# The gate and up product of a SwiGLU layer as seven half-size products per block

## The chip, the cores and the metric

The kernel runs on one core of one Trainium2 chip. The metric is device microseconds of one execution. Its median before the change is 961.82 us over three runs (961.47 to 962.75).

## The reference

One layer of a streaming encoder on 512 tokens of 1024 features, in float32. A mixing sub-layer (three attentions, merged by gates) comes first and is not touched. Then the feed-forward sub-layer, with `D_FF` = 2816:

```python
h = rmsnorm(x, g_ffn_pre[l])
gu = h @ w_ffn_in[l]
f = (jax.nn.silu(gu[..., :D_FF]) * gu[..., D_FF:]) @ w_ffn_out[l]
x = x + rmsnorm(f, g_ffn_post[l])
```

The change rewrites `h @ w_ffn_in`, a product of [512, 1024] with [1024, 5632].

## The kernel before, in words

**Numbers.** Every float32 operand is split into two parts, `hi` (a cast on ScalarE, L74) and `lo` (what is left, a subtraction on VectorE, L75; `split`). A product is three matmuls: hi by hi, hi by lo, lo by hi (`passes`, L85 to L87, called through `feat_k` and `feat`).

**Tiles.** SBUF tiles of 128x1024 come from tags with a fixed number of buffers (`BUFS`): raw weights `wraw` (3) and `lraw` (2), split weights `wh`, `wl`, `lwh`, `lwl` (2 each), `h` (8), `act` (22). `load` alternates between the tags with and without the l, `parts` makes the split pair. [...]

**The feed-forward sub-layer** (`mix_out`, `ffn`). The 2816 features are 22 blocks of 128. A pair is the gate block and the up block of the same 128 features. Its weights are two loads of 512 KB, issued from SyncE; the up block's raw tile is an `lraw`.

- `mix_out` makes the product with `w_out`, normalises the result (the chain squares on ScalarE, reciprocal root on GpSimd at L238, scaling on VectorE at L248) and transposes it to `h2`: eight blocks of 128 features with 512 tokens each, hi and lo. The transposes of the first 256 tokens are done during that product; those of the second 256 (`last_h2`) are issued between matmuls in `ffn`.
- The first three pairs (`NFIRST`) have their weights split ahead of time. `ffn` runs their products for tokens 0 to 255 first, while the norms of the last tokens finish, and then the second token half. These matmuls have 256 columns.
- The other 19 pairs run 48 matmuls of 512 columns each: two blocks, eight blocks of 128 input features, three passes.
- `finish` applies Silu on ScalarE (L819), multiplies on VectorE (L820) and splits the result at once into `fT`, the operand of the second product (`tok_pair`, L731), which streams `w_ffn_out` in 22 blocks.

**Order.** TensorE's instructions run in the order in which the program writes them. On the other engines a planner at build time orders instructions by the program's order and by when it expects their inputs and tiles to be ready; on the chip each engine's queue then runs in that order. A tile is reused when all its readers are done.

Of the kernel before, what the change touches and what calls it, by code (L numbers as in the profile page):

```python
# [35 lines left out]
# First distance of each of the 16 buckets of the relative bias.  # L36
# [3 lines left out]
def rel_onehot():  # L40
    """[32, 640] one-hot of the bucket of rel = 127 - column (a constant of the shapes)."""
    rel = 127 - np.arange(REL)
    b = np.searchsorted(np.asarray(BUCKET_START), np.abs(rel), side="right") - 1
    b = b + np.where(rel > 0, 16, 0)
    return (np.arange(32)[:, None] == b[None, :]).astype(np.float32)


class Layer:
# [32 lines left out]
    def passes(self, out, pairs, first, last):  # L81
        """out (+)= sum over pairs of (stationary hi, lo, moving hi, lo)."""
        n = len(pairs)
        for i, (sh, sl, mh, ml) in enumerate(pairs):
            self.nc.tensor.matmul(out, lhsT=sh, rhs=mh, start=first and i == 0, stop=False)  # L85
            self.nc.tensor.matmul(out, lhsT=sh, rhs=ml, start=False, stop=False)  # L86
            self.nc.tensor.matmul(out, lhsT=sl, rhs=mh, start=False, stop=last and i == n - 1)  # L87

# [1 line left out]
    def load(self, src, kc, c, tag=None):  # L90
        """src: [kc*128, c] in DRAM -> float32 tile [128, kc, c]."""
        self.nw += 1
        tag = tag or ("lraw" if self.late and self.nw % 2 else "wraw")
        raw = self.big(tag, F32)[:, :kc * c]
        self.nc.sync.dma_start(raw.rearrange("p (k c) -> p k c", c=c), src.rearrange("(k p) c -> p k c", p=P))
        return raw, c

    def parts(self, raw, tags=None, eng=None):
        """(hi, lo) tiles of a loaded tile."""
        raw, c = raw  # L100
        tags = tags or (("lwh", "lwl") if self.late and self.nw % 2 else ("wh", "wl"))
        v = [self.big(t)[:, :raw.shape[1]] for t in tags]
        self.split(*v, raw, eng)
        return [x.rearrange("p (k c) -> p k c", c=c) for x in v]
# [5 lines left out]
    def fill(self, us):  # L110
        """issue queued work of about us microseconds."""
        self.owed += us
        while self.owed > 0 and self.queue:
            try:
                self.owed -= next(self.queue[0])
            except StopIteration:
                self.queue.pop(0)
        if not self.queue:
            self.owed = 0.0

    def drain(self, *gens):
        """issue all queued work up to the last of gens (all of it without gens)."""
        while self.queue and (not gens or any(g in self.queue for g in gens)):
            self.fill(1.0)

    def mix(self, a, b, n=1):
        """b, with n steps of a after each of its steps."""
        for us in b:
            yield us + sum(next(a, 0.0) for _ in range(n))
        yield from a  # L130
# [10 lines left out]
    def feat(self, out, w, acts, kc=NK, n=T, **kw):  # L141
        """out[c, n] = w^T acts, contraction over kc*128 features."""
        for k in range(kc):
            self.feat_k(out, w, acts, k, kc, n, **kw)
            if k % 2:
                yield 1.28 * n / T
# [5 lines left out]
    # Logits of 64-dim heads: hi and lo of the queries of a head fill the 128 rows of the stationary  # L152
    # operand, against the hi part of the keys in both halves; a second pass on 64 rows has the lo part
    # of the keys. The even head keeps its hi part in the lower rows, the odd one in the upper rows.
# [23 lines left out]
    def feat_tiles(self, w_src, acts, out, js, n=T, t0=0, evac=None):  # L178
        """feature-major (hi, lo) of 128-column blocks js of w_src into out[j]."""
        per = T // n  # L180
        for j in js:
            w = self.weights(w_src[:, j * P:(j + 1) * P], NK, P)
            ps = self.bank()
            yield from self.feat(ps[:, 0:n], w, acts, n=n, t0=t0)
            if evac is not None:
                out[j] = evac(ps)
                continue
            if j % per == 0:
                slot = self.big("act")
            o = (j % per) * 2 * n  # L190
            out[j] = slot[:, o:o + n], slot[:, o + n:o + 2 * n]
            self.split(*out[j], ps[:, 0:n])

    def tok_tiles(self, w_src, acts, toks, out, heads=0):
        """token-major product with [1024, 512] weights for the token tiles toks; with heads, out[t]
        is one tile of (hi, lo) per head, side by side."""
# [23 lines left out]
    def squares(self, halves, both=False):  # L220
        """[128, 2] parts of the mean square of a row, of two halves of it; on both engines if wanted."""
# [9 lines left out]
    def rstd(self, ss):  # L231
        """-2 (mean + EPS) ** -0.5 of the two parts of the mean, with one Newton step."""
        return self.rstd2(self.rstd1(ss))
# [16 lines left out]
    def normed(self, x):  # L250
        """x * rstd(x) (gain not applied)."""
# [6 lines left out]
    def run(self):  # L258
# [4 lines left out]
        with self.tc.manual_schedule(engines={mybir.EngineType.PE}):  # L263
# [6 lines left out]
            # the first 128 queries have at most 128 admissible keys: all of them are selected  # L270
# [33 lines left out]
    def setup(self):  # L304
# [11 lines left out]
        # stick-breaking: ones where key == query, sliced per query tile  # L316
# [13 lines left out]
        # relative bias by distance, times 8  # L330
# [20 lines left out]
    def transposed(self, xs, k, g, hi, lo):  # L351
        """(hi, lo) of the transposes of columns 128k.. of the token tiles xs, times the gain g."""
# [6 lines left out]
    def first(self, x, row, w_ik, w_cq):  # L359
        """h^T by halves of the tokens, with the products of the first two weight blocks after each."""  # L360
# [88 lines left out]
    def index_keys(self, cq):  # L449
        nc = self.nc  # L450
        # shared key and head weights; first block of the queries of branch C
# [37 lines left out]
    def select(self):  # L489
        """additive masks: 0 for the 128 best admissible keys of a query, -BIG elsewhere."""  # L490
# [33 lines left out]
    def values_T(self, p, b, pT):  # L524
        """transposes of the key blocks that share bank b; p[i]: [128 queries, 128(i+1) keys]."""
# [11 lines left out]
    def values(self, pT, v, h, out):  # L537
        """out^T rows of head h = V^T P^T: V hi and lo side by side as one stationary operand."""
# [19 lines left out]
    def heads(self, prob, v, out, gap, first):  # L558
        """prob(h, i): probabilities of a query tile. The products with the values of a head come one
        head later, and queued work fills the waits."""  # L560
# [116 lines left out]
    def merge(self, b, out, wu):  # L677
        """acc (+)= sigmoid(gate of branch b) * (out @ wu), per 128 output features."""
# [38 lines left out]
    def tok_pair(self, w_src, acts, nk, toks, tail=0, keep=0):  # L717
        """[len(toks)] x 2 banks: token-major product with [nk*128, 1024] weights, streamed by k; the
        last tail blocks of k go token tile by token tile, the last keep blocks stay for the next call,
        which begins with them."""  # L720
# [32 lines left out]
    def post_norm(self, ps, grow, x, store=None):  # L753
        """x += rmsnorm(ps) * grow, for two banks."""
# [16 lines left out]
    def mix_out(self):  # L771
        nc, a = self.nc, self.a
        gp = self.grow("g_mix_post", "act")
        self.h2 = [self.pair("h") for _ in range(NK)]
# [8 lines left out]
        def to_h2(pr):  # L783
            s = slice(256 * pr, 256 * pr + 256)
            for k in range(NK):
                hi, lo = self.h2[k]
                self.transposed((xn[2 * pr], xn[2 * pr + 1]), k, 16, hi[:, s], lo[:, s])
# [18 lines left out]

    def ffn(self):
        nc, a = self.nc, self.a
        w_out = a["w_ffn_out"]
        fT = []  # L810

        def products(pss, ws, halves):
            for t0, n in halves:
                for ps, w in zip(pss, ws):
                    yield from self.feat(ps[:, t0:t0 + n], w, self.h2, t0=t0, n=n)

        def finish(pss):
            sg = self.sb.tile([P, T], F32, name="silu", tag="gate", bufs=2)
            nc.scalar.activation(sg, pss[0], AF.Silu)  # L819
            nc.vector.tensor_tensor(sg, sg, pss[1], op=OP.mult)  # L820
            hi, lo = self.pair("act")
            self.split(hi, lo, sg)
            fT.append((hi, lo))
# [3 lines left out]
        for j, w in enumerate(self.first_ffn):  # L827
            u = (self.bank(), self.bank()), w
            run(products(*u, ((0, 256),)))
            first.append(u)  # L830
        pss, ws = first[0]
        for k in range(NK + 2):
            if k < NK:
                next(self.last_h2)
            if k > 1:
                for ps, w in zip(pss, ws):
                    self.feat_k(ps[:, 256:512], w, self.h2, k - 2, n=256, t0=256)
        finish(pss)
        for u in first[1:]:
            run(products(*u, ((256, 256),)))  # L840
            finish(u[0])
        for j in range(self.NFIRST, NF):
            u = (self.bank(), self.bank()), self.ffn_weights(j)
            run(products(*u, ((0, T),)))
            finish(u[0])
# [6 lines left out]
        run(self.tok_pair(w_out, fT, NF, range(NT), tail=4))  # L852
# [18 lines left out]
```

## Time and profile before

| | |
|---|---|
| median of 3 runs | 961.82 us |
| lowest and highest run | 961.47 and 962.75 us |
| span of the profiled execution, first to last instruction | 960.9 us |
| TensorE busy | 938.7 us, 98% |
| VectorE, ScalarE, GpSimd busy | 534.3, 404.6, 107.0 us |
| the 19 pairs that are rewritten | 622.11 to 832.40 us of the span |

The profile gives no time of the profiled execution but its span, which lies 0.6 to 1.9 us under the three runs. It names engines PE (TensorE matmuls), PEld (its weight loads), DVE (VectorE), ACT (ScalarE), POOL (GpSimd) and SP (SyncE). An operation is shown as line, engine, operation, written tile, read tiles and shape; "idle before" is the time that the engine stood still before it, with what ended the wait. `bank` is a PSUM tile, all others are in SBUF.

### The profile page before, as it was taken

Reading aid. Unit: us, or ns where it says so; the run is one execution under the profiler, and the core shown is the slowest. Engines: PE = TensorE matmul, PEld = TensorE weight load, DVE = VectorE, ACT = ScalarE, POOL = GpSimd, SP = SyncE. Lnnn points to the kernel's source line nnn. Section 1 sums busy time; section 2 is a strip of 40 time slices with the busy share of each in tenths; the row PEclk is TensorE's granted clock in tenths of the full one; section 3 lists DMA queues with packets and bytes.
Section 4 is the critical chain, followed back from the end, with each engine's and each line's share of the span. In section 5 each row is a group of like instructions: output and inputs, shape, how many; then the busy total and the mean of one; then the engine's idle time right before and its main releaser. Section 6 shows DMA issues by size and latency. Waiting matters only on the chain.

```text
span 960.9 us, 11731 instructions
## 1 busy us (share of the span) xinstructions
PE 938.7 (98%) x4426; PEld 760.5 (79%) x4426; DVE 534.3 (56%) x920; ACT 404.6 (42%) x705; POOL 107.0 (11%) x147
## 2 busy tenths in 40 slices
PE   5999999999999999999999999999999999999997
PEld 4967888888777777777788888988888888888885
DVE  7568999963587876667544477333333333322225
ACT  5354575432666555655443355322223223212122
POOL 4000000010022303334222102000000000000000
PEclk9999999999999999999999999999999999999999
DMA  7423542343343322122283536023333233332202
GB/s 226 124 63 103 154 138 78 99 110 110 109 134 109 99 67 77 44 56 66 73 267 99 176 106 201 1 76 101 88 101 97 88 102 97 110 106 92 66 23 87
DMA packets 129532, 98.95 MB, mean 103 GB/s; under 512 B 4652, under 2 KB 115292, under 8 KB 129476
## 3 DMA queue, kind: packets, MB, share of 16 engines
q1 hardware_dynamic: 128884, 97.16, 33.9%
q10 hardware_dynamic: 592, 1.05, 0.3%
q8 instruction: 34, 0.56, 0.2%
q14 instruction: 22, 0.18, 0.1%
HBM read 93.73 MB, written 2.12 MB: 100 GB/s over the span
## 4 chain that ended last, share of the span: by engine, by line
PE 88%; DVE 6%; issue 2%; DMA 1%; ACT 1%; POOL 1%; SPq 0%; DVEq 0%; POOLq 0%; ACTq 0%
PE bank L85 20%; PE bank L87 20%; PE bank L86 20%; PE bank L731 14%; PE bank L176 3%; DVE wl L75 3%; PE bank L531 2%; PE bank L546 2%; PE bank L175 2%; PE bank L206 1%; PE bank L208 1%; PE bank L207 1%; DMA act<-in_x_dram 1%; DVE score L503 1%; DMA lraw<-in_w_ffn_in_dram 1%
## 5 line engine op out<-in xcount | busy, mean ns | idle before, releaser
L75 DVE TENSOR_TENSOR wl<-wraw,wh 128x1024 fp32r<-128x1024 f32 (+1 forms) x131 | 155.1, 1185 | 177.6 <-ACT wh L74 173.2
L74 ACT CAST wh<-wraw 128x1024 fp32r<-128x1024 f32 (+1 forms) x131 | 127.2, 972 | 229.4 <-PE bank L86 163.1
L85 PE MATMUL bank<-h,wh 128*128 128x512 f32 (+1 forms) x528 | 209.6, 397 | 0.0
L87 PE MATMUL bank<-h,wl 128*128 128x512 f32 (+1 forms) x528 | 204.7, 388 | 1.0 <-DVE wl L75 0.9
L86 PE MATMUL bank<-h,wh 128*128 128x512 f32 (+1 forms) x528 | 204.4, 387 | 0.0
L87 PEld LDWEIGHTS bank<-h,wl 128*128 128x128 f32 x528 | 99.1, 188 | 22.0 <-DVE wl L75 1.7
L85 PEld LDWEIGHTS bank<-h,wh 128*128 128x128 f32 x528 | 99.3, 188 | 20.0 <-issue 1.2
L86 PEld LDWEIGHTS bank<-h,wh 128*128 128x128 f32 x528 | 99.4, 188 | 17.8
L74 ACT CAST lwh<-lraw 128x1024 fp32r<-128x1024 f32 x36 | 37.9, 1052 | 119.4 <-PE bank L86 76.2
L731 PE MATMUL bank<-lwh,act 128*128 128x512 f32 x240 | 72.6, 393 | 0.0
L731 PE MATMUL bank<-wh,act 128*128 128x512 f32 x240 | 72.5, 393 | 0.0
L75 DVE TENSOR_TENSOR lwl<-lraw,lwh 128x1024 fp32r<-128x1024 f32 x36 | 44.1, 1224 | 43.1 <-ACT lwh L74 41.3
L85 PE MATMUL bank<-h,lwh 128*128 128x512 f32 x152 | 60.1, 396 | 0.0
L86 PE MATMUL bank<-h,lwh 128*128 128x512 f32 x152 | 60.1, 396 | 0.0
L87 PE MATMUL bank<-h,lwl 128*128 128x512 f32 x152 | 60.1, 395 | 0.0
L238 POOL TENSOR_TENSOR rs<-ms,mhalf 128x1 f32<-128x1 f32 x18 | 10.4, 579 | 423.9 <-DVE ms L237 419.9
L820 DVE TENSOR_TENSOR silu<-silu,bank 128x512 f32<-128x512 f32 x22 | 15.1, 686 | 76.4 <-PE bank L87 73.6
L595 POOL TENSOR_TENSOR p<-toep,score 128x128 f32<-128x128 f32 (+3 forms) x32 | 29.8, 944 | 218.4 <-DVE score L504 112.3
L731 PEld LDWEIGHTS bank<-wh,act 128*128 128x128 f32 x240 | 45.1, 188 | 10.0
L731 PEld LDWEIGHTS bank<-lwh,act 128*128 128x128 f32 x240 | 45.1, 188 | 9.9
L74 ACT CAST act<-bank 64x512 fp32r<-64x512 f32 (+3 forms) x63 | 34.8, 552 | 38.1 <-DVE act L75 16.7
L85 PE MATMUL bank<-act,wh 128*128 128x512 f32 (+1 forms) x128 | 48.6, 380 | 0.0
(161 smaller groups left out, 1616.6 us busy)
## 6 DMA issues: line engine op xcount, KB each, us to landing
wraw<-in_w_in_dram SPq DMA_DIRECT2D x64, 512.0 KB, 3.5
wraw<-in_w_ffn_in_dram SPq DMA_DIRECT2D x22, 512.0 KB, 3.7
lraw<-in_w_ffn_in_dram SPq DMA_DIRECT2D x22, 512.0 KB, 3.7
wraw<-in_w_ffn_out_dram SPq DMA_DIRECT2D x11, 512.0 KB, 3.7
lraw<-in_w_ffn_out_dram SPq DMA_DIRECT2D x11, 512.0 KB, 3.4
wraw<-in_w_mem_kv_dram SPq DMA_DIRECT2D x8, 512.0 KB, 3.4
lraw<-in_w_out_dram SPq DMA_DIRECT2D x6, 512.0 KB, 6.3
wraw<-in_w_out_dram SPq DMA_DIRECT2D x6, 512.0 KB, 4.0
```

What stands on the lines that cost most here:

```text
L74: self.nc.scalar.copy(hi, src)
L75: (eng or self.nc.vector).tensor_tensor(lo, src, hi.bitcast(F32), op=OP.subtract)
L85: self.nc.tensor.matmul(out, lhsT=sh, rhs=mh, start=first and i == 0, stop=False)
L86: self.nc.tensor.matmul(out, lhsT=sh, rhs=ml, start=False, stop=False)
L87: self.nc.tensor.matmul(out, lhsT=sl, rhs=mh, start=False, stop=last and i == n - 1)
L175: self.nc.tensor.matmul(out, lhsT=x[:, s], rhs=k[h % 2][:, 0:n], start=True, stop=False)
L176: self.nc.tensor.matmul(out, lhsT=x[r, s], rhs=lo[r, 0:n], start=False, stop=True)
L531: self.nc.tensor.transpose(ps[:, c:c + P], p[i][:, j * P:(j + 1) * P], self.ident)
L546: nc.tensor.matmul(ps[:, j * P:T], lhsT=w, rhs=part[:, o:o + n], start=j == 0 and i == 0, stop=j == NT - 1 and i == 1)
L595: nc.gpsimd.tensor_tensor(s, toep[0][:, 0:n][:, ::-1], self.mask[i], op=OP.add)
L731: self.nc.tensor.matmul(ps[c], lhsT=st_[:, s], rhs=mv_[:, 0, c * 512:(c + 1) * 512], start=f and k == order[0], stop=l and k == order[-1])
L820: nc.vector.tensor_tensor(sg, sg, pss[1], op=OP.mult)
```

## The change

For pairs 3 to 21 the two products of a pair become one block product. The inputs' features are cut into halves of 512 and the tokens into halves of 256. With g0, g1 the gate block's and u0, u1 the up block's halves by features, and q(f, t) the quarters of h, the four outputs (gate and up, for each token half) come from seven products of a combined left side (128x512 weights) with a combined right side, each of 4 blocks of 128 features, three passes and 256 columns: 84 matmuls of 256 columns instead of 48 of 512. Products 1, 2 and 4 take the weights as they are; the left sides of 5, 6, 7 and 3 are sums made on GpSimd for each pair. Products 1, 2 and 3 take quarters of h as they are; the right sides of 5, 7, 6 and 4 are made once (`right_sides`: four sums hi + lo of 128x1024 on GpSimd, then a difference and a split on VectorE and ScalarE for each). Splits come per product, into one of eight 128x1024 tiles. The partial results accumulate in three banks and are read out in between (`blocks`), and the last two products of a pair run among the first of the next: in order 1, 5, 7 (of the pair before), 2, 6, 4 (before), 3.

The layout of `h2` follows: eight `h` tiles, one per quarter and part. The result of a pair stays in float32 (two pairs in one `act` tile) and is split in the second product, when a block is first used. `passes` hands on a flag that lets a matmul add to a bank whose sum was closed before. The scratch for DMAs that GpSimd would issue is made smaller. Comments are removed, and these lines are left out of the diff.

```diff
@@ mix_out
-        self.h2 = [self.pair("h") for _ in range(NK)]
+        self.hq = {(f, t): (self.big("h"), self.big("h")) for t in range(2) for f in range(2)}
+        cut = lambda x, k: x[:, 256 * (k % 4):256 * (k % 4) + 256]
+        self.h2 = [[tuple(cut(x, k) for x in self.hq[k // 4, t]) for k in range(NK)] for t in range(2)]
...
+    def right_sides(self):
+        nc, q = self.nc, self.hq
+        r = {}
+        for k, (hi, lo) in q.items():
+            r[k] = self.big("act", F32)
+            nc.gpsimd.tensor_tensor(r[k], hi.bitcast(F32), lo.bitcast(F32), op=OP.add)
+        y = {1: q[0, 0], 2: q[1, 0], 3: q[1, 1]}
+        for p, out, x, z in ((5, (0, 0), (0, 1), (0, 0)), (7, (0, 1), (1, 1), (0, 1)),
+                             (6, (1, 1), (1, 1), (0, 0)), (4, (1, 0), (1, 0), (1, 1))):
+            nc.vector.tensor_tensor(r[out], r[x], r[z], op=OP.subtract)
+            y[p] = self.big("act"), self.big("act")
+            self.split(*y[p], r[out])
+        return y
+
+    def left_sides(self, j):
+        nc = self.nc
+        (g, _), (u, _) = (self.load(self.a["w_ffn_in"][:, c:c + P], NK, P) for c in (j * P, DFF + j * P))
+        x = {1: g[:, 0:512], 2: g[:, 512:1024], 4: u[:, 512:1024]}
+        for p, a, b, op in ((5, u[:, 0:512], x[4], OP.add), (6, 5, 1, OP.subtract),
+                            (7, x[1], u[:, 0:512], OP.subtract), (3, 2, 6, OP.subtract)):
+            a, b = (x[i] if isinstance(i, int) else i for i in (a, b))
+            x[p] = self.late.tile([P, 512], F32, name="sum", tag="sum", bufs=6)
+            nc.gpsimd.tensor_tensor(x[p], a, b, op=op)
+        return x
+
+    def product(self, out, x, y, first):
+        self.nq += 1
+        t = self.big(("wh", "lwh", "wl", "lwl")[self.nq % 4])
+        hi, lo = t[:, 0:512], t[:, 512:1024]
+        self.split(hi, lo, x)
+        for k in range(4):
+            a, b = slice(k * P, k * P + P), slice(k * 256, k * 256 + 256)
+            self.passes(out, [(hi[:, a], lo[:, a], y[0][:, b], y[1][:, b])], first and k == 0, k == 3,
+                        skip_group_check=not first)
+
+    def blocks(self, js, y, out):
+        nc = self.nc
+        half = lambda name: self.late.tile([P, 256], F32, name=name, tag=name, bufs=2)
+        def begin(j):
+            x, f = self.left_sides(j), out(j)
+            px, py, pz = (self.bank()[:, 0:256] for _ in range(3))
+            s1, s2, s3 = half("s1"), half("s2"), half("s3")
+            g = self.sb.tile([P, T], F32, name="silu", tag="gate", bufs=2)
+            self.product(px, x[1], y[1], True)
+            nc.scalar.copy(s1, px)
+            self.product(pz, x[5], y[5], True)
+            nc.scalar.copy(s3, pz)
+            yield
+            self.product(py, x[2], y[2], True)
+            nc.vector.tensor_tensor(g[:, 0:256], py, s1, op=OP.add)
+            self.product(px, x[6], y[6], False)
+            nc.scalar.copy(s2, px)
+            yield
+            self.product(pz, x[3], y[3], False)
+            nc.vector.tensor_tensor(g[:, 256:512], pz, s2, op=OP.add)
+            nc.scalar.activation(g, g, AF.Silu)
+            yield
+            self.product(px, x[7], y[7], False)
+            nc.vector.tensor_tensor(s3, px, s3, op=OP.add)
+            nc.vector.tensor_tensor(f[:, 256:512], g[:, 256:512], s3, op=OP.mult)
+            yield
+            self.product(px, x[4], y[4], False)
+            nc.vector.tensor_tensor(f[:, 0:256], g[:, 0:256], px, op=OP.mult)
+            yield
+        prev = iter(())
+        for j in js:
+            g = begin(j)
+            for _ in range(2):
+                next(g)
+                next(prev, None)
+            next(g)
+            prev = g
+        for _ in prev:
+            pass
@@ ffn
-        finish(pss)
-        for u in first[1:]:
-            run(products(*u, ((256, 256),)))
-            finish(u[0])
-        for j in range(self.NFIRST, NF):
-            u = (self.bank(), self.bank()), self.ffn_weights(j)
-            run(products(*u, ((0, T),)))
-            finish(u[0])
+        finish(pss, 0)
+        y = self.right_sides()
+        for j, u in enumerate(first[1:], 1):
+            run(products(*u, 1))
+            finish(u[0], j)
+        self.blocks(range(self.NFIRST, NF), y, out)
...
+        class Parts:
+            def __getitem__(_, k):
+                if k not in pairs:
+                    pairs[k] = self.pair("act")
+                    self.split(*pairs[k], fT[k])
+                return pairs[k]
-        run(self.tok_pair(w_out, fT, NF, range(NT), tail=4))
+        run(self.tok_pair(w_out, Parts(), NF, range(NT), tail=4))
...
-    nc = bacc.Bacc("TRN2", target_bir_lowering=False, num_devices=1)
+    nc = bacc.Bacc("TRN2", target_bir_lowering=False, num_devices=1, dynamic_dma_scratch_size=1024)
```

## Rows read from the trace of the kernel before

**Rows 1.** The page: busy time, the granted clock by slices, the chain by line.
```profile
PE 938.7 (98%) x4426; PEld 760.5 (79%) x4426; DVE 534.3 (56%) x920; ACT 404.6 (42%) x705; POOL 107.0 (11%) x147
...
PEclk9999999999999999999999999999999999999999
...
PE bank L85 20%; PE bank L87 20%; PE bank L86 20%; PE bank L731 14%; PE bank L176 3%; DVE wl L75 3%; PE bank L531 2%; PE bank L546 2%; PE bank L175 2%; PE bank L206 1%; PE bank L208 1%; PE bank L207 1%; DMA act<-in_x_dram 1%; DVE score L503 1%; DMA lraw<-in_w_ffn_in_dram 1%
```

**Rows 2.** Stretches: length, busy time (records) of PE, PEld, DVE, ACT, POOL; clock; DMA.
```profile
622.11:832.40 210.29, 210.29 (x915) 171.38 (x914) 69.80 (x75) 59.73 (x76) 0.00 (x0) 1.00 0.32 95
...
832.40:948.70 116.30, 116.22 (x507) 94.73 (x506) 31.84 (x36) 23.93 (x30) 1.09 (x2) 1.00 0.23 73
```

**Rows 3.** Timeline of VectorE, 19 pairs: start us, us, operation, idle before.
```profile
633.44 0.69 DVE L820 TENSOR_TENSOR silu<-silu,bank 128x512 f32<-128x512 f32 x1 [3.58 <-PE bank L87]
...
644.51 0.69 DVE L820 TENSOR_TENSOR silu<-silu,bank 128x512 f32<-128x512 f32 x1 [3.58 <-PE bank L87]
```

**Rows 4.** Timeline of VectorE, second token half of pairs 1 and 2.
```profile
616.62 0.69 DVE L820 TENSOR_TENSOR silu<-silu,bank 128x512 f32<-128x512 f32 x1 [2.15 <-PE bank L87]
...
622.38 0.69 DVE L820 TENSOR_TENSOR silu<-silu,bank 128x512 f32<-128x512 f32 x1 [3.69 <-PE bank L87]
```

**Rows 5.** Timeline of VectorE: two operations of 512 columns in a row.
```profile
219.76 0.69 DVE L704 TENSOR_TENSOR act<-bank,gate 128x512 f32<-128x512 f32 x1 [0.64 <-PE bank L87]
220.37 0.68 DVE L75 TENSOR_TENSOR wl<-wraw,wh 128x512 fp32r<-128x512 f32 x1
```

**Rows 6.** Groups by line and form, whole span: busy us, mean ns, idle before.
```profile
L74 ACT CAST wh<-wraw 128x1024 fp32r<-128x1024 f32 x107 | 112.3, 1051 | 206.2 <-PE bank L86 145.1 <-PE bank L731 43.1 <-issue 9.7
...
L707 POOL TENSOR_TENSOR act<-act,gate 128x512 f32<-128x512 f32 x16 | 26.9, 1684 | 61.8 <-DVE gate L706 61.8
...
L74 ACT CAST act<-silu 128x512 fp32r<-128x512 f32 x22 | 13.7, 624 | 7.2 <-DVE silu L820 7.1
...
L620 POOL TENSOR_TENSOR p<-p,e 128x512 f32<-128x512 f32 x8 | 8.7, 1092 | 13.9 <-ACT vlow L549 7.5 <-DVE e L618 6.4
...
L75 DVE TENSOR_TENSOR pt<-bank,pt 128x256 fp32r<-128x256 f32 x16 | 6.5, 406 | 1.0 <-ACT pt L74 0.9
...
L74 ACT CAST pt<-bank 128x256 fp32r<-128x256 f32 x16 | 6.0, 374 | 4.7 <-PE bank L531 4.5
```

**Rows 7.** Timelines of GpSimd and of VectorE where both work at once.
```profile
460.28 1.29 POOL L707 TENSOR_TENSOR act<-act,gate 128x512 f32<-128x512 f32 x1 [2.00 <-DVE gate L706]
...
460.37 2.29 DVE L75 TENSOR_TENSOR wl<-wraw,wh 128x1024 fp32r<-128x1024 f32 x1 [0.16 <-ACT wh L74]
...
466.76 1.23 DVE L75 TENSOR_TENSOR wl<-wraw,wh 128x1024 fp32r<-128x1024 f32 x1
...
466.89 2.25 POOL L707 TENSOR_TENSOR act<-act,gate 128x512 f32<-128x512 f32 x1
...
581.71 2.42 POOL L75 TENSOR_TENSOR act<-lraw,act 128x1024 fp32r<-128x1024 f32 x1 [2.34 <-ACT act L74]
...
582.62 0.69 DVE L760 SCALAR_TENSOR_TENSOR prod<-bank,act 128x512 f32<-128x512 f32 x1
```

**Rows 8.** Timelines of VectorE and TensorE before the 19 pairs.
```profile
585.27 0.48 DVE L79 SCALAR_TENSOR_TENSOR h<-bank,cols,h 128x256 fp32r<-128x256 f32 x1
...
597.78 0.75 DVE L248 TENSOR_SCALAR act<-fin,rs 128x1024 f32<-128x1024 f32 x1
...
602.02 0.60 PE L356 MATMUL bank<-ident,act 128*128 128x128 f32 x4
...
609.15 0.48 DVE L79 SCALAR_TENSOR_TENSOR h<-bank,cols,h 128x256 fp32r<-128x256 f32 x1 [0.45 <-ACT h L78]
```

**Rows 9.** Timeline of TensorE at a wait, and the stretch after it.
```profile
585.34 0.39 PE L86 MATMUL bank<-h,act 128*128 128x256 f32 x1 [1.38 <-DVE h L79]
...
586.00:589.40 3.40, 3.40 (x18) 3.40 (x18) 3.40 (x6) 3.40 (x10) 0.00 (x0) 0.52 0.37 109
```

**Rows 10.** DMA issues of the page: count, KB each, median us to landing.
```profile
wraw<-in_w_ffn_in_dram SPq DMA_DIRECT2D x22, 512.0 KB, 3.7
```

More of the change, by code (lines that the diff above doesn't have):

```diff
@@ L79, in split_gain, with passes @@
         self.nc.vector.scalar_tensor_tensor(lo, src, g, hi.bitcast(F32), op0=OP.mult, op1=OP.subtract)
-    def passes(self, out, pairs, first, last):
+    def passes(self, out, pairs, first, last, **kw):
         n = len(pairs)
         for i, (sh, sl, mh, ml) in enumerate(pairs):
-            self.nc.tensor.matmul(out, lhsT=sh, rhs=mh, start=first and i == 0, stop=False)
-            self.nc.tensor.matmul(out, lhsT=sh, rhs=ml, start=False, stop=False)
-            self.nc.tensor.matmul(out, lhsT=sl, rhs=mh, start=False, stop=last and i == n - 1)
+            self.nc.tensor.matmul(out, lhsT=sh, rhs=mh, start=first and i == 0, stop=False, **kw)
+            self.nc.tensor.matmul(out, lhsT=sh, rhs=ml, start=False, stop=False, **kw)
+            self.nc.tensor.matmul(out, lhsT=sl, rhs=mh, start=False, stop=last and i == n - 1, **kw)
     def load(self, src, kc, c, tag=None):
@@ L783, in to_h2 @@
         def to_h2(pr):
-            s = slice(256 * pr, 256 * pr + 256)
             for k in range(NK):
-                hi, lo = self.h2[k]
-                self.transposed((xn[2 * pr], xn[2 * pr + 1]), k, 16, hi[:, s], lo[:, s])
+                self.transposed((xn[2 * pr], xn[2 * pr + 1]), k, 16, *self.h2[pr][k])
                 yield 0.25
@@ L809, in ffn, with out, products, finish @@
         w_out = a["w_ffn_out"]
[L810 to L817, printed above, removed]
+        fT, self.nq = [], 0
+        def out(j):
+            if j % 2 == 0:
+                self.slot = self.big("act", F32)
+            fT.append(self.slot[:, (j % 2) * T:(j % 2 + 1) * T])
+            return fT[j]
+        def products(pss, ws, t):
+            for ps, w in zip(pss, ws):
+                yield from self.feat(ps[:, 256 * t:256 * t + 256], w, self.h2[t], n=256)
+        def finish(pss, j):
             sg = self.sb.tile([P, T], F32, name="silu", tag="gate", bufs=2)
             nc.scalar.activation(sg, pss[0], AF.Silu)
[L820 to L823, printed above, removed]
+            nc.vector.tensor_tensor(out(j), sg, pss[1], op=OP.mult)
         run = lambda g: [None for _ in g]
@@ L828, in ffn @@
             u = (self.bank(), self.bank()), w
-            run(products(*u, ((0, 256),)))
+            run(products(*u, 0))
             first.append(u)
@@ L836, in ffn @@
                 for ps, w in zip(pss, ws):
-                    self.feat_k(ps[:, 256:512], w, self.h2, k - 2, n=256, t0=256)
-        finish(pss)
-        for u in first[1:]:
-            run(products(*u, ((256, 256),)))
-            finish(u[0])
-        for j in range(self.NFIRST, NF):
-            u = (self.bank(), self.bank()), self.ffn_weights(j)
-            run(products(*u, ((0, T),)))
-            finish(u[0])
+                    self.feat_k(ps[:, 256:512], w, self.h2[1], k - 2, n=256)
+        finish(pss, 0)
[4 more added lines that the diff above has]
+        self.blocks(range(self.NFIRST, NF), y, out)
         gp = self.grow("g_ffn_post", "h")
@@ L851, in ffn @@
         self.done = done
-        run(self.tok_pair(w_out, fT, NF, range(NT), tail=4))
+        pairs = {}
+        class Parts:
[5 more added lines that the diff above has]
+        run(self.tok_pair(w_out, Parts(), NF, range(NT), tail=4))
 def kernel(**inputs):
-    nc = bacc.Bacc("TRN2", target_bir_lowering=False, num_devices=1)
+    nc = bacc.Bacc("TRN2", target_bir_lowering=False, num_devices=1, dynamic_dma_scratch_size=1024)
     arrays = {}
```

## Prediction

> **What bounds the kernel now.** I read the page's busy shares and its clock line first: TensorE is busy for 98% of the span, VectorE for 56%, GpSimd for 11%, and the granted clock is 0.9 or more in every slice [rows 1]. Then the chain of waits: the three lines of `passes` (L85 to L87), the body of every feature-major product, carry 60% of it [rows 1]. Then the stretches: the 19 pairs that the change rewrites take 210.29 us, from 622.11 to 832.40, with TensorE busy for all of it, VectorE for 69.80, ScalarE for 59.73 and GpSimd for nothing [rows 2]. So in this stretch one column of TensorE work removed is time removed, as long as the three other engines keep pace. Those queues, not TensorE, decide what the change is worth.
>
> One pair takes 11.07 us: the multiply that ends it (L820) starts at 633.44 and at 644.51 [rows 3], and 210.29/19 gives the same. A pair is 2 x 8 x 3 = 48 matmuls of 512 columns, so one costs 11.07/48 = 0.231 us.
>
> **What the change removes on TensorE.** Seven products, each of 4 blocks of k by 3 passes, are 84 matmuls of 256 columns. The trace has their price: pairs 1 and 2 do their second token half in 48 such matmuls each, and their closing multiplies start at 616.62 and 622.38 [rows 4], so one costs 5.76/48 = 0.120 us. A pair costs 84 x 0.120 = 10.08 us, 0.99 less than now. Seven eighths of the columns would give 1.38; the smaller matmul has more overhead per column (0.120 for half of 0.231), which takes back 0.39. If nothing else binds, 19 pairs gain 18.8 us. The weight loads go with the matmuls: in that stretch they have the same pitch, so they are in the 0.120.
>
> **What it adds on the other engines, per pair.** VectorE: seven `lo` subtractions of 512 columns (now two of 1024 in the pair), and five operations of 256 columns: three additions and one multiply that read PSUM, one multiply that reads SBUF alone. A 512 operation shows 0.69 us, but the next starts 0.61 after it [rows 5]; the 256 one shows 0.406 [rows 6], less the same 0.08 is 0.33. Sum: 7 x 0.61 + 5 x 0.33 = 5.92 us, against 69.80/19 = 3.67 now. ScalarE: seven casts at 0.62, three PSUM copies at 0.37 and one Silu at about 0.62 [rows 6] are 6.1 us, against 3.14 now; that lies under 10.08. Loads stay two of 512 KB a pair.
>
> GpSimd gets four sums of 128x512. The cheapest such group is 1.09 (a multiply), the dearest mean is 1.68 [rows 6], which contains waiting; a sum that started without a wait shows 1.29, and half of the 1024 subtraction (2.42) is 1.21 [rows 7]. I take 1.28, by the first: 5.12 us a pair.
>
> 5.92 and 5.12 look small beside 10.08, but they exclude each other in part. Rows 7 show it. A `lo` subtraction of 1024 takes 1.23 when it comes first (466.76); started 0.09 after a GpSimd sum it took 2.29, and it ended 1.09 after the sum's end (462.66 against 461.57). The other way round, the sum that met the subtraction of 466.76 took 2.25 for its 1.29, and ended 1.15 after it. While GpSimd ran for 2.42 us from 581.71, the VectorE operation at 582.62 that reads a PSUM bank kept its usual 0.69. So VectorE work with both inputs in SBUF and GpSimd work take turns; VectorE work with a PSUM input does not. [...]
>
> VectorE's queue is my main term. [...] If no GpSimd work lies beside VectorE work, a pair needs 5.92 + 5.12 = 11.04 us; if all four PSUM-reading operations (1.32) lie beside a sum, 9.72. The middle is 10.38, which is over TensorE's 10.08. Nothing in rows says how well the planner packs them, and the seven subtractions outnumber the four operations that can overlap, so I take 10.38: a gain of 0.69 a pair, 13.1 us for 19. The ends are 11.04 (gain 0.6 in all) and the bound by TensorE (18.8). Eight tiles for split sides let the splits run up to eight products (11.5 us) ahead, which can hide part of a deficit of 0.30 x 19 = 5.7 us; how full that store is at the start depends on the next part.
>
> **Edits at the edges.** (a) `right_sides` puts four GpSimd sums of 1024 (2.42 each) in the queue that also makes the reciprocal root of the mix's last norms. Two of them are ready when the first token half is split (585.7), in the middle of the chain through three such roots to the scaled rows at 598.53; TensorE has other products until 602.02 [rows 8]. Two sums in front cost that chain 4.84 at most, the slack is 602.02 - 598.53 = 3.5: 0 to 1.3 us, I take 0.5. (b) The second half is complete at 609.63 [rows 8]. From there the first made side needs a sum, a difference, a cast and a subtraction (2.42 + 1.23 + 1.05 + 1.23 = 5.9 [rows 6, 7], with the other sum ahead of it 8.3), so it is ready by 618, and product 5 starts at 622.11 + 1.44 = 623.5: hidden. The third made side (product 6) needs both sums and six VectorE operations, 12.2 us, plus the first blocks' splits and sums between them (up to 5 x 0.61 + 4 x 1.28 = 8.2): 622 to 630 against 626.4. 0 to 3.6, I take 1. This also leaves the store half full. (c) After the last pair, products 7 and 4 follow each other with a VectorE addition from their bank between: 0.41 and two hand-overs, 0.5. (d) The 22 splits of the product's result move into the second FFN product, where VectorE is busy for 31.84 of 116.30 and ScalarE for 23.93 [rows 2]: 22 x 0.69 and 22 x 0.62 fit, cost 0; uncovered, the first would cost 1.3 once. (e) The new layout of h2, the matmul flag, the smaller scratch (no DMA is issued from GpSimd) and the removed comments: 0. Edges: 2.0.
>
> Sum: 961.8 - 13.1 + 2.0 = 950.7, say **951**. The profiled execution's span is 960.9, the runs 961.47 to 962.75; the sum is a difference and I lay it on the median.
>
> **The rivals.** *TensorE stays fed* (the store and the overlap suffice): 961.8 - 18.8 + 0 to 2 = 943 to 945. For it: with the best packing the two engines need 9.72 of 10.08. Against: that is 96% of the time, with jitter.
>
> *No overlap*: 11.04 a pair, 961.8 - 0.6 + 2 = 963, no change. For it: the stretched subtraction waited for almost the whole sum. Against: it needs every PSUM-reading operation to fall outside the sums.
>
> [...]
>
> *The lookahead is not there.* The `u` block's raw tile has two buffers and is held until the split for product 4, six places into the next pair's order. [...]
>
> **Chances.** The forecast, 10.2 to 10.9 a pair with the edges (947 to 960): 0.50. TensorE fed: 0.25. No overlap: 0.10. Clock: 0.10. No lookahead: 0.05. The range takes in the fed case and most of the no-overlap case, 942.5 to 964. A measurement of this kernel can tell about 0.2% (1.9 us) from no change. Faster: 0.50 + 0.25 + about 0.05 of the others = 0.80; same: 0.07 (the middle of no overlap); slower: 0.13 (the clock, most of the lookahead case).
>
> **What would show it.** In the profile after: TensorE's 256-column matmuls at a pitch of 0.120, and seven products per pair; the pair's period from its last multiply between 10.08 and 10.9; `lo` subtractions of 512 stretched to 1.2 to 1.9 in every pair, beside GpSimd sums; TensorE waiting for VectorE's `lo` by some tenths of a us per pair; clock 0.9 throughout. The prediction is wrong if the sums are much cheaper or dearer than 1.28, if TensorE waits for ScalarE or for a load, if the wait sits at the start (622 to 630), or if the clock falls inside the 19 pairs.

## The result and the profile after

The median after is 1011.08 us (1010.01 to 1011.57) against 962.23 us before on the same chip: a ratio of 1.0514, interval 1.0499 to 1.0529. The forecast of 951 and its range were wrong, and so was the sign. The profiled execution took 1010.88 us with a span of 1009.1, 48.2 more than the span before.

The page after, busy time, granted clock, and the chain of waits by engine and by line; it answers to [rows 1]:

```profile
PE 939.6 (93%) x5110; PEld 797.2 (79%) x5110; DVE 650.2 (64%) x1099; ACT 461.6 (46%) x861; POOL 229.1 (23%) x227
...
PEclk9999999999999999999999998988999998999999
...
PE 62%; DVE 14%; DMA 9%; issue 8%; POOL 4%; ACT 3%; POOLq 0%; DVEq 0%; SPq 0%; ACTq 0%
PE bank L731 14%; PE bank L85 12%; PE bank L87 11%; PE bank L86 11%; DMA lraw<-in_w_ffn_in_dram 9%; DVE wl L75 3%; PE bank L176 3%; POOL sum L839 3%; PE bank L531 2%; PE bank L546 2%; DVE lwl L75 2%; PE bank L175 1%; DVE wh L75 1%; DVE lwh L75 1%; PE bank L206 1%
```

TensorE has less of the chain now, 62%. The lines of `passes` had 60% of it and now have 34%; the loads of the `u` blocks into `lraw` have 9%, the GpSimd sums 3%, and VectorE 14% (here `g` and `u` are the gate and the up block of a pair). Stretches of the kernel after come next (length, then busy time and records of TensorE, its weight loads, VectorE, ScalarE, GpSimd; granted clock; DMA): up to the transposes of the second token half, from there to the first block product, and the 19 pairs.

```profile
580.00:611.29 31.29, 21.86 (x155) 20.24 (x153) 26.23 (x37) 12.61 (x30) 21.26 (x16) 0.92 0.26 77
...
611.29:632.18 20.89, 20.89 (x157) 20.89 (x157) 11.92 (x15) 9.86 (x14) 4.77 (x2) 0.88 0.02 4
...
632.18:880.54 248.36, 208.16 (x1598) 204.50 (x1597) 160.07 (x232) 106.93 (x214) 101.04 (x68) 0.93 0.29 85
```

The first two of them in the kernel before, with the same TensorE work:

```profile
580.00:603.49 23.49, 20.99 (x155) 19.97 (x153) 15.50 (x33) 11.68 (x26) 4.58 (x5) 0.93 0.56 163
...
603.49:622.11 18.62, 18.62 (x157) 18.62 (x158) 6.00 (x11) 7.16 (x12) 0.00 (x0) 1.00 0.00 1
```

So the 48.2 us have three places. Before the second half's transposes 31.29 - 23.49 = 7.80; from there to the pairs 20.89 - 18.62 = 2.27, in which TensorE is busy throughout, with the same 157 matmuls, at a lower granted clock (0.88 against 1.00); and 37.9 in the pairs: 248.36 against 210.4 by the same bounds ([rows 2] end at the last multiply, 0.13 earlier). The rest, from the second FFN product's first matmul to the end, is 128.6 against 128.4.

**Where the pairs lose.** TensorE is idle for 40.2 of the 248.36 us. These are the waits of the kernel after around the pairs (us in all, times, longest):

```profile
POOL sum L839 <- DMA lraw<-in_w_ffn_in_dram: 138.7, 17, 19.8
...
PE bank L85 <- DVE s L879: 40.2, 18, 4.0
```

TensorE stops once a pair, for an addition on VectorE (L879); GpSimd stops once a pair, for the load of the `u` block. The chain of waits shows one turn (start, us, what):

```profile
718.26 5.10 DMA lraw<-in_w_ffn_in_dram
...
723.53 1.27 POOL sum L839
...
724.82 0.63 ACT wh L74
...
726.61 1.75 DVE lwh L75
...
731.31 0.60 DVE wh L75
...
731.94 4.66 DMA lraw<-in_w_ffn_in_dram
```

It goes from load to load, and TensorE is not in it. VectorE's timeline shows what stands between the first split that needs the load and the split that lets the next load start; its first line is the same last split one turn earlier:

```profile
717.56 0.68 DVE L75 TENSOR_TENSOR lwh<-lraw,lwh 128x512 fp32r<-128x512 f32 x1
...
725.47 1.21 DVE L75 TENSOR_TENSOR wh<-sum,wh 128x512 fp32r<-128x512 f32 x1 [5.37 <-ACT wh L74]
726.61 1.75 DVE L75 TENSOR_TENSOR lwh<-sum,lwh 128x512 fp32r<-128x512 f32 x1
728.28 0.41 DVE L879 TENSOR_TENSOR s<-bank,s 128x256 f32<-128x256 f32 x1
728.62 1.42 DVE L75 TENSOR_TENSOR wl<-wraw,wl 128x512 fp32r<-128x512 f32 x1
729.97 0.41 DVE L880 TENSOR_TENSOR act<-silu,s 128x256 f32<-128x256 f32 x1
730.30 0.41 DVE L870 TENSOR_TENSOR silu<-bank,s 128x256 f32<-128x256 f32 x1
730.63 0.68 DVE L75 TENSOR_TENSOR lwl<-sum,lwl 128x512 fp32r<-128x512 f32 x1
731.23 0.68 DVE L75 TENSOR_TENSOR wh<-lraw,wh 128x512 fp32r<-128x512 f32 x1
```

From 725.47 on, the L75 rows are the splits for product 5 of pair y, 7 of the pair before it (x), 2 and 6 of y, and last (731.23, the only one of this turn that reads `lraw`) product 4 of x. Product 4's split is the last reader of x's `u` tile, one of two, and the load into that tile is issued at 731.94. The split for product 5 of y (725.47) could not run before y's `u` block had landed. So each load waits for a split that stands in VectorE's queue behind splits that wait for the load before it: one load per turn, in a circle. The turn is load and hand-over 5.27 (718.26 to 723.53), sum and cast 1.94 (to 725.47), VectorE's rows 6.44 (to 731.91), issue 0.03: 13.68. The closing multiplies (L883) at 650.35 and 865.58 are 16 turns apart, 13.45 each on average.

The matmul that TensorE resumes with after the turn's stop is product 4's, and its own split was ready 10.5 us earlier (VectorE's row of 717.56). It waited for L879, which reads the bank that product 4 writes, and which stood in VectorE's queue behind the two late splits. The last matmul that L879 needs, product 7's, had ended at 722.46, and VectorE was idle up to 725.47; L879 still ran in its place, at 728.28:

```profile
728.75 0.39 PE L85 MATMUL bank<-act,lwh 128*128 128x256 f32 x1 [3.44 <-DVE s L879]
...
728.75:732.50 3.75, 3.75 (x18) 3.75 (x19) 3.74 (x7) 0.62 (x1) 0.74 (x1) 0.54 0.30 84
```

After the stop the granted clock is 0.54, for 18 matmuls. Inside the circle that costs nothing: the chain of the turn does not go through TensorE, which needs 10.04 of the 13.45 us when it is fed (second experiment).

### The profile page after: what moved, and what is told of

Read it like the earlier page. It is cut to its first block, busy times and chain, and to the rows that moved or that the text cites. A ratio compares the mean times of both kernels' runs of the same rounds, so it can differ in the third digit from the quotient of the medians.

```text
span 1009.1 us, 13643 instructions
## 1 busy us (share of the span) xinstructions
PE 939.6 (93%) x5110; PEld 797.2 (79%) x5110; DVE 650.2 (64%) x1099; ACT 461.6 (46%) x861; POOL 229.1 (23%) x227
## 4 chain that ended last, share of the span: by engine, by line
PE 62%; DVE 14%; DMA 9%; issue 8%; POOL 4%; ACT 3%; POOLq 0%; DVEq 0%; SPq 0%; ACTq 0%
PE bank L731 14%; PE bank L85 12%; PE bank L87 11%; PE bank L86 11%; DMA lraw<-in_w_ffn_in_dram 9%; DVE wl L75 3%; PE bank L176 3%; POOL sum L839 3%; PE bank L531 2%; PE bank L546 2%; DVE lwl L75 2%; PE bank L175 1%; DVE wh L75 1%; DVE lwh L75 1%; PE bank L206 1%
## 5 line engine op out<-in xcount | busy, mean ns | idle before, releaser
L75 DVE TENSOR_TENSOR wl<-wraw,wh 128x1024 fp32r<-128x1024 f32 (+1 forms) x112 | 131.8, 1178 | 102.8 <-ACT wh L74 98.3
L85 PE MATMUL bank<-h,wh 128*128 128x512 f32 (+2 forms) x432 | 167.2, 387 | 0.0
L87 PE MATMUL bank<-h,wl 128*128 128x512 f32 (+2 forms) x428 | 161.3, 377 | 1.0 <-DVE wl L75 0.9
L86 PE MATMUL bank<-h,wh 128*128 128x512 f32 (+2 forms) x432 | 161.5, 374 | 0.0
L85 PEld LDWEIGHTS bank<-h,wh 128*128 128x128 f32 x432 | 82.7, 191 | 13.7 <-issue 1.2
L86 PEld LDWEIGHTS bank<-h,wh 128*128 128x128 f32 x432 | 82.6, 191 | 11.6
L85 PE MATMUL bank<-act,wh 128*128 128x256 f32 (+1 forms) x204 | 71.1, 348 | 6.7 <-DVE s L879 6.7
L87 PE MATMUL bank<-act,wl 128*128 128x256 f32 (+1 forms) x208 | 69.6, 335 | 0.0
L86 PE MATMUL bank<-act,wh 128*128 128x256 f32 (+1 forms) x204 | 68.5, 336 | 0.0
L839 POOL TENSOR_TENSOR sum<-lraw 128x512 f32<-128x512 f32 x19 | 24.9, 1312 | 138.9 <-DMA lraw<-in_w_ffn_in_dram 138.9
L85 PEld LDWEIGHTS bank<-act,wh 128*128 128x128 f32 x204 | 39.2, 192 | 13.0 <-DVE s L879 7.5
L75 DVE TENSOR_TENSOR lwl<-lraw,lwh 128x1024 fp32r<-128x1024 f32 x17 | 21.3, 1254 | 36.5 <-ACT lwh L74 36.4
L620 POOL TENSOR_TENSOR p<-p,e 128x128 f32<-128x128 f32 (+3 forms) x32 | 24.3, 760 | 86.3 <-DVE e L618 43.9
```

Of the source, the lines that this page charges most:

```text
L75: (eng or self.nc.vector).tensor_tensor(lo, src, hi.bitcast(F32), op=OP.subtract)
L620: nc.gpsimd.tensor_tensor(be, be, e[:, 1:n + 1], op=OP.mult)
L839: nc.gpsimd.tensor_tensor(x[p], a, b, op=op)
```

## Experiments

The first theory is the circle. It has two rivals. The port theory, as the expectations call it, is that VectorE's subtractions and GpSimd's sums take turns: in the turn above the splits beside sums took 1.21, 1.75 and 1.42 us, the others 0.68. Only the longer times are measured; no run shows what makes the two engines take turns. The clock theory is that TensorE at a low clock (0.54 after the stop) holds the pair up. For the start the theory is that GpSimd's sums delay the last norms.

**A third buffer for `u`.** The tags swap, so that `u` has three raw tiles and `g` two. Every engine keeps the same instructions.

```diff
-        (g, _), (u, _) = (self.load(..., NK, P) for c in (j * P, DFF + j * P))
+        (g, _), (u, _) = (self.load(..., NK, P, t) for c, t in ((j * P, "lraw"), (DFF + j * P, "wraw")))
```

> The up block's raw tile takes the tag with three buffers and the gate block's the one with two; nothing else changes, every engine has the same instructions. Loop theory: the 13.45 us of a pair are a circle: the load of an up block waits for a free raw tile, which product 4's lo subtraction frees; that subtraction stands in VectorE's queue behind the next pair's subtraction for product 5, which waits for the next up load. With a third buffer two pairs share a turn of the circle, so the pair falls to 10.1 to 10.9 us and the kernel to 1011 - 18 x 2.8 = about 960 (954 to 966). Port theory: the GpSimd sums and VectorE's subtractions take turns and need 13.45 us a pair by themselves: same instructions, so 1011 within 3. [...]

965.08 us (963.57 to 966.99). The kernel before, run beside it, took 961.17; the ratio is 1.0039 (1.0026 to 1.0052). The pairs of this kernel:

```profile
637.34:834.77 197.43, 191.81 (x1598) 190.08 (x1597) 175.92 (x232) 106.26 (x214) 99.51 (x65) 1.00 0.36 107
```

One buffer more takes 50.9 us out of the pairs (10.39 each) and 46 off the run. The same sums stand beside the same subtractions, so neither the turns that the two engines take nor the amount of VectorE work is enough to make the 13.07. By the clock theory the pairs would have kept their time too; here the granted clock is 1.00. TensorE still waits 5.6 us in seven places, and the start is worse: the pairs begin at 637.34.

**Product 4's split earlier.** The split is written after product 3 of its own pair, ahead of the next pair's splits; no buffer is added. `halves` is the first part of `product`, set apart.

```diff
             self.product(pz, x[3], y[3], False)
+            x4 = self.halves(x[4])
...
-            self.product(px, x[4], y[4], False)
+            self.product(px, x4, y[4], False)
```

> Only the place of product 4's split changes: it is written right after product 3 of its own pair, ahead of the next pair's products 1 and 5, so that VectorE frees the up block's raw tile before it waits for the next up load. Buffers, engines and TensorE's order stay. Loop theory: as with the third buffer, 10.1 to 10.9 us a pair, kernel about 960 (954 to 966). Port theory and clock theory: 1011 within 4.

948.84 us in one run. The same kernel once more, with several runs:

> The early split of product 4 alone, timed in rounds: 948.8 within 2, as in its one look; 19 pairs at 190.8 us with VectorE and GpSimd taking turns all the same.

947.26 us (946.39 to 948.47), ratio 0.9860 (0.9843 to 0.9876) to 961.0: the fastest version of this study, faster than both kernels. Its pairs, and three rows of its VectorE timeline (product 4's split, the next pair's product 5, product 4's again):

```profile
625.83:816.65 190.82, 189.99 (x1599) 189.79 (x1597) 176.10 (x231) 110.52 (x216) 104.81 (x66) 1.00 0.36 107
...
704.39 1.45 DVE L75 TENSOR_TENSOR wl<-lraw,wl 128x512 fp32r<-128x512 f32 x1
...
705.95 1.60 DVE L75 TENSOR_TENSOR wh<-sum,wh 128x512 fp32r<-128x512 f32 x1
...
715.23 1.45 DVE L75 TENSOR_TENSOR lwh<-lraw,lwh 128x512 fp32r<-128x512 f32 x1
```

The split that frees the tile now precedes the one that waits for the next load, and the circle is open. TensorE is busy for 189.99 of 190.82: 10.04 a pair, its own bound. Its one stop comes after the last pair's product 7 (0.83 us at 815.11). It keeps this pace although the subtractions are still stretched (1.45 and 1.60 for 0.69) and GpSimd is busy for 104.81. Moving one split in the program, with the order that the planner makes of it, was worth 57.5 us of pairs.

The run gained 63.8, so 6.3 more came from the start, where the edit changes nothing that the program asks for. In this kernel GpSimd makes the sums of `right_sides` behind the last norms and not among them. The two VectorE operations behind the last root, those sums (L821), and the stretch from the transposes to the pairs:

```profile
604.40 0.22 DVE L243 SCALAR_TENSOR_TENSOR rt<-rs,ms 128x1 f32<-128x1 f32 x1 [0.45 <-POOL rs L238]
604.66 0.16 DVE L244 SCALAR_TENSOR_TENSOR rs<-rt,rs 128x1 f32<-128x1 f32 x1
...
609.13 9.48 POOL L821 TENSOR_TENSOR act<-h 128x1024 f32<-128x1024 f32 x4
...
607.21:625.83 18.62, 18.62 (x157) 18.62 (x157) 12.85 (x15) 9.20 (x14) 11.33 (x6) 1.00 0.02 5
```

What this says of the start is taken up below.

**The sums on VectorE.** GpSimd has nothing left in the pairs; the order and the buffers are those of the change.

```diff
-            nc.gpsimd.tensor_tensor(x[p], a, b, op=op)
+            nc.vector.tensor_tensor(x[p], a, b, op=op)
```

> The four sums of a pair run on VectorE in place of GpSimd; two buffers for the up block as in the change. Loop theory: the circle stays (load about 5, then sums at 0.6, cast, subtractions without stretches), so the pair still takes 11.3 to 12.5 us, kernel 975 to 992. Port theory: nothing excludes VectorE any more, its work is 5.9 + 2.4 = 8.4 us a pair, so TensorE is the bound at 10.1 us and the kernel falls to 945 to 955.

969.55 us in one run: between the two expectations, nearer the circle's and below its range.

```profile
627.72:838.79 211.07, 194.80 (x1599) 191.54 (x1597) 160.44 (x300) 107.50 (x215) 0.00 (x0) 0.99 0.34 100
...
753.73 0.69 DVE L839 TENSOR_TENSOR sum<-lraw 128x512 f32<-128x512 f32 x1 [2.01 <-DMA lraw<-in_w_ffn_in_dram]
```

The circle is still there: now VectorE itself waits for the load, once a pair, and a pair takes 11.11. But it is 1.96 shorter a pair than with GpSimd. So the turns between VectorE and GpSimd are no cause by themselves, but they lengthen the circle: the GpSimd sum, its hand-over and the stretched subtractions are links of it. This run does not tell them apart.

**Three `u` buffers and every sum on VectorE**, those of `right_sides` too:

```diff
-            nc.gpsimd.tensor_tensor(r[k], hi.bitcast(F32), lo.bitcast(F32), op=OP.add)
+            nc.vector.tensor_tensor(r[k], hi.bitcast(F32), lo.bitcast(F32), op=OP.add)
```

and the edits of the first and third experiments.

> Three buffers for the up block, and all sums (those of the pairs and the four of the right sides) on VectorE. Loop theory and port theory agree: the pair at TensorE's 10.1 us, and with no GpSimd work among the norms before the pairs the stretch starts at about 622 to 626 as before, so the kernel takes 943 to 952. If it stays above 962, neither theory has the cause.

957.19 us (956.45 to 959.26), ratio 0.9959 (0.9945 to 0.9973). It misses what both theories expected, in the pairs and at the start. Its stretch ahead of the pairs, and the pairs:

```profile
606.98:628.37 21.39, 21.39 (x157) 21.39 (x157) 12.95 (x17) 7.92 (x12) 0.00 (x0) 0.86 0.02 3
...
628.37:828.90 200.53, 193.57 (x1598) 190.31 (x1597) 162.34 (x299) 111.37 (x216) 0.00 (x0) 1.00 0.36 106
```

A pair takes 10.55, not 10.1: TensorE waits 6.7 us in 13 places, and VectorE's sums wait for the loads of `u` for 31.5 us in 16, with everything behind them. With three buffers the place of the sums changes little in the pairs (10.39 on GpSimd, in the first experiment); with two, VectorE was the better place (11.11 against 13.07). The pairs begin 9.0 us earlier than in the first experiment, and the run is 7.9 shorter. But the start of the kernel before did not come back: the 157 matmuls from 606.98 on took 21.39 us at clock 0.86, against 18.62 at 1.00.

**Keeping the sums out of the norms.** Two gates are tried with the early split, and the first of them on the change alone too. The first ties the loads of the pairs' first blocks to the last normed rows: a VectorE operation writes one column of the raw tile, which the load then overwrites. The second lets them load and ties their sums to those rows (first pair) or to the last split of h2 (next two): it adds zero times a value to one column of the weights. The first gate, without the lines that choose the loads:

```diff
         raw = self.big(tag, F32)[:, :kc * c]
+        if after is not None:
+            self.nc.vector.tensor_copy(raw[:, 0:1], after[:, 0:1])
```

> Two edits to the change: product 4's split early (as in the run of that edit alone), and the raw tiles of pairs 3 and 4 and of pair 5's gate block get one column from the last normalised rows before their load, so that no sum or split of the pairs can run among the norms. Start theory: the pairs began 5.6 to 15 us late because planned-ahead sums and splits stood in GpSimd's, VectorE's and ScalarE's queues among the last norms and the h2 splits; without them the first pair starts at 622 to 625 (622.11 before), the pairs take 190.8, the rest 128.4, so the kernel takes 942 to 946. Rival: the late start comes from the new layout of h2 or from the right sides, which stay: 948 to 950, as with the early split alone.

952.12 us (951.56 to 953.62), ratio 0.9911 (0.9896 to 0.9925): slower than without the gate (947.26).

> The change with the gated loads alone; product 4's split stays late. The circle through the up block's raw tile stays, so the pairs take 245 to 252 us. Start theory: first pair at 622 to 626 in place of 632.18, kernel 1001 to 1006. Rival (start held by the right sides): 1008 to 1012.

1007.94 us in one run; the pairs took 247.51, as expected with the circle, and began at 630.12.

The second gate, again the operation alone:

```diff
+                    nc.vector.scalar_tensor_tensor(raw[:, c:c + 1], z[:, 0:1], 0.0, raw[:, c:c + 1], op0=OP.mult, op1=OP.add)
```

> Product 4's split early as before; the loads of the first pairs stay early too, but a one-column operation that leaves the weights as they are makes their sums and splits wait: pair 3 for the last normalised rows, pairs 4 and 5 for the last split of h2. Start theory: the norms end near 595, as with the gated loads, and now only pair 3's six splits and four sums lie in the gap before the h2 splits, so TensorE waits under 2 us there in place of 9.34; first pair at 622 to 624, pairs 190.8, kernel 941 to 945. Rival: the right sides and the later sums collide after the h2 splits and the wait moves into the pairs: 946 to 950.

958.12 us (957.03 to 958.82), ratio 0.9965 (0.9953 to 0.9977). TensorE's waits at the start, first in the load gate's kernel, then in the sum gate's:

```profile
609.52 0.48 PE L358 MATMUL bank<-ident,act 128*128 128x128 f32 x1 [9.34 <-DVE h L79]
```

```profile
606.68 0.69 PE L356 MATMUL bank<-ident,act 128*128 128x128 f32 x2 [4.21 <-DVE h L79]
...
622.73 9.38 POOL L821 TENSOR_TENSOR act<-h 128x1024 f32<-128x1024 f32 x4
...
634.32 0.58 PE L85 MATMUL bank<-act,wl 128*128 128x256 f32 x1 [5.22 <-ACT act L74]
```

All three missed their times. With the loads gated the norms were done by 595.1, and TensorE's first stop, at 584.38, fell to 0.51 us; but the loads, sums and splits then stood in front of the splits of h2, and TensorE waited 9.34. With the sums gated, the four sums of `right_sides` ran behind sums of the pairs, 14 us later than with the early split alone (622.73 against 609.13), and a product waited 5.22 for them. The wait moved each time; no version here has the start of the kernel before (622.11; the nearest is 625.83). Which order would do it stays open.

## Why the prediction was wrong

**TensorE's part was right.** 84 matmuls at 0.120 were to be 10.08 a pair; the kernel with the early split measures 10.04 with one stop of TensorE. The 18.8 us are there: its pairs are 19.6 shorter than before.

**The main term was of the wrong kind.** The prediction took VectorE's queue and its turns with GpSimd as a rate, 10.38 a pair as the middle of 9.72 and 11.04. As a rate they do not bind: the kernel with the early split runs at 10.04, TensorE's own pace, with stretched subtractions in every pair. So the no-overlap rival (11.04) is wrong too, and "TensorE stays fed" had the pairs right once the circle was gone. What bound was a latency: 13.45 a turn, in which VectorE is idle for 5.37 us at a stretch.

**The step that failed** is how the lookahead was counted. The rival *The lookahead is not there* had found the tile with two buffers and the split that holds it, and got 0.05, because lookahead was counted in split tiles alone: "Eight tiles for split sides let the splits run up to eight products (11.5 us) ahead". The splits did run that far ahead (10.5 us for product 4), and it did not help: what held the load back was the place of that split in VectorE's queue, behind splits that wait for the load before. The step asked how far ahead of TensorE the split is, and should have followed the queue from a load to the next load. The third buffer alone took 2.7 us a pair off, and the earlier split 3.0.

**The edges (a) and (b)** were sized at 1.5 together and measured 10.07. For (b) no stop of TensorE in the pairs is put down to a made side, so (a) has it all. It counted two sums of `right_sides` on GpSimd's queue. The rows show more: the scaled rows end at 609.68, against 598.53 before, because the splits and sums of the first pairs also stand between the norms, and because VectorE's own small operations were held up. The last root and the sums beside it in the kernel after, with TensorE's wait:

```profile
604.22 4.66 POOL L821 TENSOR_TENSOR act<-h 128x1024 f32<-128x1024 f32 x2
...
604.28 2.32 DVE L243 SCALAR_TENSOR_TENSOR rt<-rs,ms 128x1 f32<-128x1 f32 x1 [0.45 <-POOL rs L238]
606.63 2.26 DVE L244 SCALAR_TENSOR_TENSOR rs<-rt,rs 128x1 f32<-128x1 f32 x1
608.93 0.75 DVE L248 TENSOR_SCALAR act<-fin,rs 128x1024 f32<-128x1024 f32 x1
...
609.74 0.90 PE L356 MATMUL bank<-ident,act 128*128 128x128 f32 x3 [4.40 <-DVE act L248]
```

and the same two operations before:

```profile
597.34 0.22 DVE L243 SCALAR_TENSOR_TENSOR rt<-rs,ms 128x1 f32<-128x1 f32 x1 [0.66 <-POOL rs L238]
597.59 0.16 DVE L244 SCALAR_TENSOR_TENSOR rs<-rt,rs 128x1 f32<-128x1 f32 x1
```

Two sums cost this chain 4.2 us through VectorE, not through GpSimd's queue, where (a) put them. The kernel with the early split is the test of it. The step behind its last root starts 0.12 us later than here (604.40), but with the sums behind the norms the same two operations take 0.22 and 0.16. TensorE then has no such wait, and takes 18.62 us from there to the pairs, as before. So 632.18 - 625.83 = 6.35 of the 10.07 are the place of these two sums, the fall of the clock included.

The other 3.72 lie ahead of the transposes, which begin at 607.21 in that kernel, against 603.49 before. TensorE has an earlier stop there, in the kernel after 3.45 us:

```profile
587.62 0.39 PE L86 MATMUL bank<-h,act 128*128 128x256 f32 x1 [3.45 <-DVE h L79]
```

It is 3.24 with the early split and 1.38 in the kernel before [rows 9]. With the loads of the first pairs gated it was 0.51, so it comes from the first pairs' work among the norms, which (a) did not count. Behind the stop the clock is lower too, 0.87 from 580.00 to 607.21 with the early split against 0.93 up to 603.49 before. How much each of those sums and splits has in the 3.72 is not shown.

**The clock**, to which the prediction gave 0.10, counted in another place. It fell in the pairs, to 0.54 over the 18 matmuls after the stop shown above, and cost nothing there, since the circle set the pace (TensorE's busy time in the pairs is 208.16, against 189.99 with the early split, and it still waits for 40.2). It did cost at the start, 2.27 us (0.88 against 1.00), where TensorE had waited 4.40 and then was busy up to the pairs.

**The other edges** held: nothing for the splits moved into the second FFN product (0.2 us for the whole rest), and for (c), the turn of products 7 and 4 after the last pair, TensorE waited 0.68 us here (at 879.05) and 0.83 with the early split, against 0.5.

## What to carry to other kernels

For every tile that is loaded in a loop, follow the in-order queues from the landing of one load to the issue of the next: if the tile's last reader stands behind an instruction that waits for the next block, the loop has the latency of a load in every turn, however many buffers the stage behind it has (here 13.45 us a turn). Here it opened the circle to write the last reader ahead of that instruction, with no buffer and no instruction more (10.04); a further buffer opened it nearly as well (10.39). A rate computed from busy times (5.92 and 5.12 beside 10.08) says nothing of this. For a loop, estimate two times, the work of its busiest engine and the longest circle of waits from one turn to the next; the larger one sets the pace.

## What the hardware showed beyond that

- A VectorE operation on 128x1 with its inputs in SBUF took 2.32 and 2.26 us beside GpSimd sums of 2.33 (4.66 for two), against 0.22 and 0.16 alone. Here the wait followed the other engine's instruction, not the size of the waiting one.
- With VectorE at 176.10 and GpSimd at 104.81 busy in 190.82 us, waiting for each other included, TensorE lost 0.8 us in all, and that after the last pair's product 7.
- The load of 512 KB into `lraw` took 4.66 and 5.10 us in the circle's turns. It was issued 1.84 us after the load of `g` (716.42 and 718.26), while that one was under way. The sum that waits for it started 5.24 us after the issue (723.50). With the early split the two loads are 5.08 and 5.04 us apart (the second ones issued at 705.86 and 716.70), and the sums started 3.88 and 4.20 us after those issues; in the kernel before the median to landing is 3.7. No run changes the spacing alone.
- After a wait of 4.40 us TensorE took 20.89 us for 157 matmuls (granted clock 0.88) that took 18.62 at 1.00 in the kernel before and with the early split.
